# Writing out TensorE's order in the RWKV recurrence, the dilated attention and the gates of a two-block network

## The chip, the cores and the metric

The kernel runs on one core of a Trainium2 chip. The metric is the device time of one execution in microseconds (us). The kernel before has a median of 924.59 us over three runs (924.24 to 924.65).

## What is computed

The network maps 256 tokens of 1024 channels through two blocks. The first is an even layer (pooling and spatial gating) and an odd layer (gated linear attention and stick-breaking attention). The second block, where the change lies, is cut down here to its mixing part:

```python
u = rmsnorm_2(h, mix_pre_norm[i])
z = u @ w_in[i]
z_attn, z_rwkv, z_gate = ...
o_attn = dilated_attention_branch(z_attn)
o_rwkv = rwkv7_time_mix(z_rwkv, ...)
gate_attn, gate_rwkv = jnp.split(jax.nn.sigmoid(z_gate), 2, axis=-1)
merged = gate_attn * (o_attn @ w_attn_up[i]) + gate_rwkv * (o_rwkv @ w_rwkv_up[i])
h = h + rmsnorm_2(merged @ w_out[i], mix_post_norm[i])
```

`rwkv7_time_mix` is a recurrence over 256 steps for 8 heads of 64; after it come a feed-forward layer and a gated embedding (PLE), which the change leaves alone.

## The kernel before

Every dense product is done in three: a float32 weight tile of 128x1024 is split into a high part `whi` (ScalarE) and a low part `wlo` (VectorE), the activation likewise, and `acc_T` (line 398) issues high x high, high x low and low x high for each block of 128 channels. These three matmuls are called a gate step below when they belong to the gates. The gates need 16 tiles of 8 steps, 384 matmuls. A weight tile comes by a DMA of 512 KB on SP's queue (`weights`, line 367); there are three buffers each of `whi` and `wlo`, so a split also waits for the last matmul of the tile three before it.

The recurrence is done in four chunks of 64 tokens. `gram` (line 1645) makes 64x64 products of keys, queries and decay vectors, masked on VectorE into the tiles `G`. The chunk's triangular system is inverted by `inverse` (line 1809), for two groups of four heads: the innermost 16x16 blocks are solved in `bl` by a chain of small VectorE operations and come back through DRAM as `tb`; `tt` and its transpose `tn` are made from it on VectorE; then TensorE does tn x G, P1 x tt, and again on 32x32 blocks tn x G and tt x P1, with a copy of each result `P1` between. Then `rwkv` (line 1630) walks the four chunks: U, the state S, and on every second one the output Y, which is normalised, transposed and turned into the split tiles `mhl`.

The dilated attention (`attention`, line 1928) works for two query blocks j and two head pairs i: scores, a softmax (`sc`: exp, then scaling by the reciprocal sum, both on ScalarE), transposes of the weights, their copies `aPT`, and the product with the values into `o_ps`.

What sets the order: generators that yield after each piece, woven by ratios. Attention and gates are woven into `fill` by RA and RB, and `fill` into the recurrence by RC and RD (lines 239 and 1236). That is the order of issue only; each engine's program is then ordered by the scheduler from its own model. `keep_in_program_order` takes an instruction out of its hands, and is used for some operations elsewhere (`o`, line 311). After the recurrence, a loop (line 1239) does for each of 8 tiles 6 matmuls of attn_up and 12 of rwkv_up, and merges them under the gates.

## Time and profile before

| what | value |
| --- | --- |
| median of three runs | 924.59 us (924.24 to 924.65) |
| the profiled execution | 924.33 us |
| its span, first to last instruction | 922.6 us |
| mean granted TensorE clock, share of full speed | 0.986 |
| TensorE (PE) busy | 890.4 us, 97% of the span |
| VectorE (DVE) busy | 687.0 us, 74% |
| ScalarE (ACT) busy | 505.1 us, 55% |
| GpSimd (POOL) busy | 58.8 us, 6% |

The profiled execution's own time is 1.73 us longer than its span; this is what lies around the first and last instruction. PEld in the page is the loading of TensorE's weights, which overlaps its products. [...] All times of rows count from the start of the span.

## The change

TensorE's instructions of the recurrence, the attention and the gates are issued through `pe`, which keeps them in the order of the program while `first` is set. The generators' ratios go; instead `rwkv` calls `fill(a=, g=, u=)` by hand, which takes so many pieces of attention, of gates and of attn_up. A piece of the gates is one step (`gemm_fine`), and the next weight tile is asked for when a tile begins. It is `nc.tensor` calls beside `mm` that now go through `pe` too. The inverse yields after each half of its products, and two gate steps go there (one behind the last). Both head pairs' scores of a query block come first, then transposes and products; the product's accumulator comes from the other PSUM pool. attn_up moves into the loop of the last transposes, and the gate tile is overwritten in place.

```diff
-        self.nc.tensor.matmul(out, lhsT, rhs, start=start, stop=stop)
+        self.pe(self.nc.tensor.matmul(out, lhsT, rhs, start=start, stop=stop))
+
+    def pe(self, ins):
+
+        if self.first:
+            self.tc.keep_in_program_order(ins)
...
+    def gemm_fine(self, prefix, n, xs, evac):
+
+        w = self.weights(prefix + "0", NK)
+        for i in range(n):
+            acc = self.psum(T, prefix)
+            ahead = self.weights(prefix + str(i + 1), NK) if i + 1 < n else None
+            for k in range(NK):
+                self.acc_T(acc, w, xs[k:k + 1], 0, P, k0=k, first=k == 0, last=k == NK - 1)
+                if k == NK - 1:
+                    evac(i, acc)
+                yield
+            w = ahead
...
-        fill = self.weave(self.attention(qkv, o_at), self.gemm_T("gate", 16, us, ev_gate), RA, RB)
-        self.run(self.weave(self.rwkv(rw, o_rw), fill, RC, RD))
-        ms, wa = [], None
+        wa = []
+
+        def attn_up():
+
+            for i in range(8):
+                if i % 4 == 0:
+                    wa.append(self.weights("attn_up%d" % (i // 4), 2))
+                pa = self.psum(T, "up")
+                self.acc_T(pa, wa[-1], o_at, (i % 4) * P, (i % 4 + 1) * P)
+                self.stt(gates[i], gates[i], 1.0, pa, ALU.add, ALU.mult)
+                yield
+
+        att, gate, up = self.attention(qkv, o_at), self.gemm_fine("gate", 16, us, ev_gate), attn_up()
+
+        def fill(**n):
+            for g, name in ((att, "a"), (gate, "g"), (up, "u")):
+                for _ in range(n.get(name, 0)):
+                    next(g, None)
+
+        self.first = True
+        self.rwkv(rw, o_rw, fill)
+        fill(a=99, g=999, u=9)
+        self.first = False
...
-        yield from grams("ab", B, A, strict)
-        G = pre["ab"]
+        G = gram(B, A, strict)
...
-        for name, X, Y, mask in (("ak", K, A, strict), ("rb", B, R, causal)):
-            for _ in grams(name, X, Y, mask):
-                yield
-                yield
+        fill(a=2, g=4)
+        pre["ak"] = gram(K, A, strict)
+        fill(a=2, g=8)
+        fill(a=3)
+        pre["rb"] = gram(B, R, causal)
+        fill(g=4)
+        fill(a=1, g=4)
...
-            yield
-        for _ in range(NX):
-            yield
-        yield from self.weave(self.inverse(0, G, tb, TT[0]), self.inverse(1, G, tb, TT[1]), 1, 1)
+            fill(a=1, g=2)
+        fill(a=1, g=14)
+        for n, _ in enumerate(self.weave(*(self.inverse(hh, G, tb, TT[hh]) for hh in range(2)), 1, 1)):
+            fill(g=2 if n < 8 else 1)
...
-                yield
+                fill(g=3)
...
+                    if M is Kt:
+                        fill(g=2)
...
-            yield
+            fill(u=2)
...
         ps = self.pmisc((P, 8, 16))
         for m, g in M:
             for b in range(0, P, 32):
                 self.mm(ps[q(b), m, :], g[q(b), q(b % 64)], tn[q(b), m, 0:16], True, True)
+            if m % 4 == 3:
+                yield
...
+            s_of = []
             for i in range(2):
                 sc = self.b4("sc", 512)
                 ss = [sc[:, hh, 0:2 * n] for hh in range(2)]
-                mxs = scores(j, i, ss)
-                for hh in range(2):
-                    weights(ss[hh], mxs[hh])
-                    yield
-
-
+                for s, mx in zip(ss, scores(j, i, ss)):
+                    weights(s, mx)
+                s_of.append(ss)
+                yield
+            for i, ss in enumerate(s_of):
+
+
+                pts = []
                 for g in range(2):
                     nb, w = (2, m) if g else (j + 1, P)
                     ps = self.pmisc((P, 4, P))
                     bs = [(b, hh) for b in range(nb) for hh in range(2)]
                     for k, (b, hh) in enumerate(bs):
-                        nc.tensor.transpose(ps[0:w, k, :], ss[hh][:, g * n + b * w:g * n + (b + 1) * w], ident)
+                        self.pe(nc.tensor.transpose(ps[0:w, k, :], ss[hh][:, g * n + b * w:g * n + (b + 1) * w], ident))
                     pt = self.m2("aPT", (P, 4, P))
                     self.act(pt[0:w, 0:len(bs), :], ps[0:w, 0:len(bs), :])
+                    pts.append((pt, w, bs))
```

In the order of TensorE, at the start of the inverse (rwlev_pm is its accumulator, tn and P1 its operands, gate the accumulator of a gate tile), there stood before

```order
L309 MATMUL rwch_gate_1438_7390<-gla_hl_944_4590,rwch_wlo_1441_7394 128x256
L309 MATMUL rwlev_pm_1392_6999<-rwlev_tn_1389_6992,rwlev_G_1288_6464 32x16 x32
L309 MATMUL rwlev_pm_1394_7034<-rwlev_tn_1391_6996,rwlev_G_1289_6466 32x16 x32
L309 MATMUL rwlev_pm_1404_7110<-rwlev_P1_1393_7032,rwlev_tt_1388_6991 32x16 x32
L309 MATMUL rwlev_pm_1406_7146<-rwlev_P1_1395_7067,rwlev_tt_1390_6995 32x16 x32
L309 MATMUL rwlev_pm_1408_7182<-rwlev_tn_1389_6992,rwlev_G_1288_6464 32x32 x16
L309 MATMUL rwch_gate_1438_7390<-gla_hl_955_4645,rwch_whi_1440_7393 128x256 x2
L309 MATMUL rwlev_pm_1410_7206<-rwlev_tn_1391_6996,rwlev_G_1289_6466 32x32 x16
```

and now

```order
L309 MATMUL rwlev_gate_1414_7096<-gla_hl_955_4645,rwlev_whi_1411_7065 128x256 x2
L309 MATMUL rwlev_gate_1414_7096<-gla_hl_955_4645,rwlev_wlo_1412_7066 128x256
L309 MATMUL rwlev_pm_1420_7113<-rwlev_tn_1419_7110,rwlev_G_1288_6464 32x16 x16
L309 MATMUL rwlev_pm_1423_7134<-rwlev_tn_1422_7131,rwlev_G_1289_6466 32x16 x16
L309 MATMUL rwlev_gate_1414_7096<-gla_hl_968_4704,rwlev_whi_1411_7065 128x256 x2
L309 MATMUL rwlev_gate_1414_7096<-gla_hl_968_4704,rwlev_wlo_1412_7066 128x256
L309 MATMUL rwlev_gate_1414_7096<-gla_hl_981_4763,rwlev_whi_1411_7065 128x256 x2
L309 MATMUL rwlev_gate_1414_7096<-gla_hl_981_4763,rwlev_wlo_1412_7066 128x256
L309 MATMUL rwlev_pm_1420_7113<-rwlev_tn_1419_7110,rwlev_G_1288_6464 32x16 x16
L309 MATMUL rwlev_pm_1423_7134<-rwlev_tn_1422_7131,rwlev_G_1289_6466 32x16 x16
```

Four products of 32 rows that stood one behind the other are now eight of 16, with two gate steps behind each pair.

On VectorE, at the same place (gt is the evacuation of a finished gate tile, wlo the low part of a weight tile, tt and tn the operands of the inverse), there stood before

```order
L331 TENSOR_TENSOR rwlev_tt_1388_6991<-rwlev_tb_1356_6797,cst2_5133 128x256
L1823 STREAM_TRANSPOSE rwlev_tn_1389_6992<-rwlev_tt_1388_6991 128x256
L331 TENSOR_TENSOR rwlev_tt_1390_6995<-rwlev_tb_1356_6797,cst2_5133 128x256
L1964 RECIPROCAL rwlev_tn_1398_7073<-rwlev_tn_1397_7071 128x1
L1823 STREAM_TRANSPOSE rwlev_tn_1391_6996<-rwlev_tt_1390_6995 128x256
L331 TENSOR_TENSOR rwch_wlo_1472_7604<-rwch_wst_1470_7601,rwch_whi_1471_7603 128x1024
```

and now

```order
L336 TENSOR_TENSOR rwlev_gt_1413_7093<-rwlev_gate_1409_7062,rbc_u_5099 128x256
L336 TENSOR_TENSOR rwlev_tt_1418_7109<-rwlev_tb_1374_6843,cst2_5133 128x256
L1851 STREAM_TRANSPOSE rwlev_tn_1419_7110<-rwlev_tt_1418_7109 128x256
L336 TENSOR_TENSOR rwlev_tt_1421_7130<-rwlev_tb_1374_6843,cst2_5133 128x256
L336 TENSOR_TENSOR rwlev_wlo_1432_7278<-rwlev_wst_1430_7275,rwlev_whi_1431_7277 128x1024
L1851 STREAM_TRANSPOSE rwlev_tn_1422_7131<-rwlev_tt_1421_7130 128x256
```

An evacuation of a gate tile now stands ahead of the first tt, and a split of a weight tile between the second tt and its transpose.

On ScalarE, ahead of the last products of the inverse (P1 is their operand, TT the finished inverse), there stood before

```order
L343 ACTIVATE rwlev_TT_1284_6423<-rwlev_tt_1405_7144 32x8x32 x2
L343 ACTIVATE rwlev_P1_1409_7199<-rwlev_pm_1408_7182 32x256
L343 ACTIVATE rwlev_TT_1284_6423<-rwlev_tt_1405_7144 32x8x32 x2
L343 ACTIVATE rwlev_P1_1411_7223<-rwlev_pm_1410_7206 32x256
L343 ACTIVATE rwlev_TT_1285_6424<-rwlev_tt_1407_7180 32x8x32 x4
```

and now

```order
L348 ACTIVATE rwlev_TT_1285_6424<-rwlev_tt_1434_7291 32x8x32 x4
L348 ACTIVATE rwch_whi_1459_7487<-rwch_wst_1458_7485 128x1024
L348 ACTIVATE rwlev_gt_1437_7345<-rwlev_gt_1437_7345 128x256
L348 ACTIVATE rwlev_P1_1438_7348<-rwlev_pm_1435_7299 32x256
L348 ACTIVATE rwlev_P1_1440_7364<-rwlev_pm_1436_7308 32x256
```

The split whi_1459 and the tanh of a gate tile stand ahead of the two copies of P1. On VectorE the other half of the same place is now

```order
L336 TENSOR_TENSOR rwlev_gt_1437_7345<-rwlev_gate_1429_7274,rbc_u_5099 128x256
L336 TENSOR_TENSOR rwch_wlo_1460_7488<-rwch_wst_1458_7485,rwch_whi_1459_7487 128x1024
L1879 COPY rwlev_P1_1438_7348<-rwlev_pm_1435_7299 32x256
L1879 COPY rwlev_P1_1440_7364<-rwlev_pm_1436_7308 32x256
```

so that the low part of that same weight tile stands ahead of the copies into P1 there. The two splits write the buffers that gate tile 1429 reads, whose last matmul stands on TensorE directly ahead of tt x P1.

## Rows read from the trace of the kernel before

**Rows 1.** The page: TensorE's busy time, and its granted clock in 40 slices.

```profile
PE 890.4 (97%) x7228; PEld 828.3 (90%) x7228; DVE 687.0 (74%) x1284; ACT 505.1 (55%) x863; POOL 58.8 (6%) x120
...
PEclk7999999999999999999999999899999999999998
```

**Rows 2.** Windows: length, busy us of PE, PEld, DVE, ACT, POOL; clock, DMA share, GB/s.

```profile
588.00:590.00 2.00, 0.86 (x66) 0.65 (x65) 1.77 (x6) 1.25 (x2) 0.00 (x0) 1.00 0.80 233
...
592.00:594.00 2.00, 0.16 (x11) 0.16 (x13) 0.13 (x1) 0.83 (x2) 0.00 (x0) 0.95 0.83 248
594.00:600.00 6.00, 6.00 (x88) 5.65 (x84) 2.02 (x5) 4.25 (x10) 0.00 (x0) 0.50 0.02 5
600.00:602.00 2.00, 2.00 (x21) 1.69 (x21) 0.42 (x1) 0.78 (x1) 0.00 (x0) 0.84 0.00 0
```

**Rows 3.** All waits of TensorE, 540 to 672 us: total us, times, longest.

```profile
PE rwlev_pm L309 <- issue: 1.9, 1, 1.9
PE rwlev_pm L309 <- DVE rwlev_tn L1823: 1.1, 1, 1.1
PE rwlev_pm L1984 <- ACT rwlev_sc L343: 0.3, 1, 0.3
PE rwch_pm L1798 <- DVE rwch_Y L331: 0.3, 1, 0.3
```

**Rows 4.** TensorE's timeline, 578 to 602 us: start, length, operation, count, idle before.

```profile
578.53 2.08 PE L1643 MATMUL rwlev_pm<-rw_tok,rwlev_G 64*64 64x64 f32 x64
...
585.83 0.40 PE L309 MATMUL rwlev_gate<-gla_hl,rwlev_whi 128*128 128x256 f32 x2
...
586.19 0.40 PE L309 MATMUL rwlev_gate<-gla_hl,rwlev_whi 128*128 128x256 f32 x2
...
589.24 1.47 PE L309 MATMUL rwlev_pm<-rwlev_tn,rwlev_G 32*32 32x16 f32 x126 [1.10 <-DVE rwlev_tn L1823]
...
590.58 1.32 PE L309 MATMUL rwlev_pm<-rwlev_P,rwlev_tt 32*32 32x16 f32 x120
593.84 0.24 PE L309 MATMUL rwlev_pm<-rwlev_P,rwlev_tt 32*32 32x16 f32 x3 [1.95 <-issue]
...
595.59 1.07 PE L309 MATMUL rwlev_pm<-rwlev_tn,rwlev_G 32*32 32x32 f32 x32
...
597.71 0.63 PE L309 MATMUL rwch_gate<-gla_hl,rwch_whi 128*128 128x256 f32 x2
...
598.35 0.63 PE L309 MATMUL rwch_gate<-gla_hl,rwch_whi 128*128 128x256 f32 x2
...
601.94 1.20 PE L309 MATMUL rwlev_pm<-rwlev_tt,rwlev_P 32*32 32x32 f32 x64
```

**Rows 5.** VectorE's timeline, 588 to 596 us.

```profile
588.19 0.43 DVE L331 TENSOR_TENSOR rwlev_tt<-rwlev_tb,cst 128x256 f32<-128x256 f32 x1 [0.99 <-DMA rwlev_tb<-td]
588.65 0.45 DVE L1823 STREAM_TRANSPOSE rwlev_tn<-rwlev_tt 128x256 f32<-128x256 f32 x1
...
589.80 1.18 DVE L331 TENSOR_TENSOR rwch_wlo<-rwch_wst,rwch_whi 128x1024 fp32r<-128x1024 f32 x1
...
595.38 0.43 DVE L1847 COPY rwlev_P<-rwlev_pm 32x256 f32<-32x256 f32 x1 [0.42 <-ACT rwlev_P L343]
```

**Rows 6.** ScalarE's timeline, 583 to 599 us.

```profile
583.30 0.72 ACT L343 ACTIVATE rwlev_sc<-rwlev_sc,rwlev_tn 128x512 f32<-128x512 f32 x1 [2.05 <-DVE rwlev_tn L335]
...
584.88 1.06 ACT L343 ACTIVATE rwch_whi<-rwch_wst 128x1024 fp32r<-128x1024 f32 x1 [0.45 <-ACT rwlev_gt L343]
...
594.97 0.38 ACT L343 ACTIVATE rwlev_P<-rwlev_pm 32x256 f32<-32x256 f32 x1 [1.91 <-PE rwlev_pm L309]
...
598.81 0.60 ACT L343 ACTIVATE rwlev_aPT<-rwlev_pm 128x512 f32<-128x512 f32 x1
```

**Rows 7.** Around TensorE's wait in w_out: its row on the timeline, and the window.

```profile
688.86 0.39 PE L309 MATMUL rwch_w_out<-rwch_hl,rwch_wlo 128*128 128x256 f32 x1 [1.18 <-DVE rwch_wlo L331]
...
686.00:692.00 6.00, 4.82 (x41) 4.62 (x40) 5.65 (x11) 4.15 (x8) 0.00 (x0) 1.00 0.83 264
```

## What the change was predicted to do

> **What bounds the kernel now.** I read the page first: TensorE is busy for 890.4 of the 922.6 us, 97%, and the row of its granted clock is full in all slices but three [rows 1]. So time is won or lost only where TensorE waits, or where it works at its lower clock. The change touches only the stretch from about 549 us (first product of the recurrence) to the start of w_out. I therefore read that stretch by windows, then the list of TensorE's waits in it, then the timelines of TensorE, VectorE and ScalarE around the place where something is lost.

> The windows show one weak place, 588 to 602 us: in 588:590 TensorE has 0.86 us of work, in 592:594 only 0.16, and the clock is 0.50 in all of 594:600 [rows 2]. With the parts in 592:594 (0.95) and 600:602 (0.84) the half clock lasted 0.2 + 6.0 + 0.64 = 6.84 us. The waits name the rest: 1.1 us for a transpose of VectorE, 1.9 us put down to "issue", 0.3 for a scaled score tile, 0.3 for Y [rows 3]. Nothing else waits between 540 and 672. On TensorE's timeline these are the start of the 64x64 inverse at 589.24 (after 1.10), its 246 small products in two bursts without a gate between them, the 1.95 us before 593.84, and gate matmuls that come at half pace from 597.71 on [rows 4].

> **What goes away.** The total of TensorE's products does not change, only their order.
> - The two bursts (126 and 120 records, 589.24 to 591.9) are cut into pieces with two gate steps between them, so that TensorE no longer has hundreds of very short instructions in a row. I count the whole 1.95 us "issue" idle as gone; its bounds are 0 and 1.95. [...]
> - The 1.10 us wait for the transpose is replaced by the wait (c) below: 1.10 gone.
> - The 0.3 us wait for the scaled scores [rows 3]: gone, since the second pair of score products now stands ahead of the transposes.
> - The half clock. A gate step of three matmuls took 0.64 us there (597.71 to 598.35) and takes 0.36 at full clock (585.83 to 586.19) [rows 4]. In the 6.84 us TensorE did 17 gate matmuls (17/3 x 0.28 = 1.6 us lost) and two lots of 32 of the 32x32 products (1.07 per 32 at 595.59 against 1.20 per 64 at 601.94: 0.9), and four transposes, which I put at 0.3 as an estimate from the same ratio. That is 2.8; bounds 1.6 (gates alone) and 3.4 (half of 6.84).

> Together 1.95 + 1.10 + 0.3 + 2.8 = 6.2 us.

> **What the fixed order adds.** TensorE now runs in the written order, but VectorE and ScalarE still get theirs from the scheduler, and in it the splitting of the next gate weight tile often stands ahead of a small step of the inverse. The third weight buffer is free only when the last matmul of an earlier gate tile is done, so such a split is tied to TensorE's own progress.
> - (c) The first products of the inverse. On VectorE stand, behind the end of gate tile 1409: gt_1413, tt_1418, the transpose tn_1419, tt_1421, then wlo_1432, and only then the transpose tn_1422. By [rows 5] a tt is 0.43 and a transpose 0.45, and gt has the shape of tt: head 0's operand is there 1.3 us after the tile's end, while TensorE has two gate steps (0.72) to do: 0.6 wait. After these four VectorE has wlo_1432, 1.2 (whi_1431, 1.06 on ScalarE [rows 6], is done by then), and the transpose, 0.45: head 1's operand is there 1.3 + 0.3 + 1.2 + 0.45 = 3.25 after the tile's end (0.3 is the step of tt_1421, which overlaps). TensorE gets there at 0.72 + 0.6 + 0.3 = 1.6: another 1.6 wait. Sum 2.2; bounds 1.1 (as before) and 3.
> - (d) The last products of the inverse. whi_1459 waits for the last matmul of gate tile 1429, which is the instruction just ahead of tt x P on TensorE; P1_1438 needs both ScalarE, behind whi_1459, and VectorE, behind wlo_1460. So TensorE stands for whi 1.06 + wlo 1.2 + copy 0.43 = 2.7 us [rows 5, 6]. Nothing covers it. Bounds 1.4 (the ScalarE half alone: 1.06 + 0.38) and 3.2.
> - (b) The j = 1 product of attention, o, wants two aPT copies (0.60 each) on ScalarE, behind four exps and scales of the second score pair (0.72 each), whi_1411 (1.06) and two AKV copies (as large as aPT, 0.60 each) [rows 6]. From the end of the second score pair TensorE has 36 + 12 gate matmuls (5.8 us), the two halves of AKV (2.08 at 578.53) and eight transposes (an estimate of 0.8, a gate matmul's 0.12 each and a little less): 8.7. ScalarE has 4 x 0.72 + 1.06 + 4 x 0.60 = 6.3 of its own, and it starts only when VectorE has the maxima; the 2.05 us of idle before such a row [rows 6] is what that costs, with as much again between exp and scale. That is 10.4, so 1.7 more than TensorE has; bounds 0 and 3.
> - Two small ones: the second pair of scores waits for both G copies to free its accumulators, and the first rwkv_up product waits for its split operand: 0.7 together, bounds 0 and 1.5.
> - At no cost: the weight loads of SP are as many and in the same order, with three buffers, so each is issued when its buffer is free as before; attn_up (48 matmuls) only moves from behind the last transposes to between them, and what it covers there is the 0.3 wait for Y, which the new order still has ahead of the first transposes. If that cover were gone, 0.3 at each of the three later transposes.

> Added: 2.2 + 2.7 + 1.7 + 0.7 = 7.3.

> **The sum.** 924.33 us (profiled execution: span 922.6 and 1.73 around it) - 6.2 + 7.3 = 925.4. The profiled run lies 0.26 below the median of 924.59, so on the scale of the medians it is 925.7. A measurement of this kernel can tell about 0.2%, 1.85 us, from no change, so this is "same", near its upper edge. Its own spread by the bounds is some 2 us either way.

> **Rivals.**
> *The clock falls at the new stalls.* Before, it fell after 5.7 us (588.14 to 593.84) in which TensorE had only small products and two idle times (1.10 and 1.95) [rows 4], and did not at a plain idle time of 1.18 (688.86, clock 1.00 in 686:692) [rows 7]. The 2.7 of (d) is longer than any of these, and (c) makes 2.2 in three pieces with small products between. [...] Against it: at (c) and (d) full-size gate matmuls stand right before and after. One fall costs what it cost before, 2.8: 928.5; two, 931.3. It decides at one of the two stalls being long enough. Chance 0.27.

> *The waits are mostly covered: faster.* If ScalarE reaches the aPT copies in time (b = 0), if the split at (c) is done before head 1 asks (0.7 instead of 2.2), and if (d) is only the ScalarE half (1.4), the order adds 0.7 + 0.7 + 1.4 = 2.8 against 6.2 removed: 924.59 - 3.4 = 921.2. For it: before, VectorE idled 0.99 and ScalarE 2.05 around the same steps [rows 5, 6], so they have room. Against it: the two splits are tied to a matmul that stands directly ahead, so their chain can't start earlier. It turns on where these two splits stand when the weight buffer comes free. Chance 0.30.

> *The order is not what costs.* The stalls move only, and the inverse again waits about 3 us in all, with the half clock as before: 924.6. Chance 0.05. It would need the gate steps to make no difference between the bursts.

> **How the numbers follow.** Forecast 0.38, 925.7, own range 924 to 928. Faster by over 0.2% (below 922.7): most of the second rival and a little of the forecast, 0.30. Within: half of the forecast, the third rival and the edges of the others, 0.30. Slower (above 926.4): the rest of the forecast and nearly all of the first rival, 0.40. The range goes from 920.0 (the second rival less 1.2, about half the half clock's own bounds) to 930.0 (the first rival with one fall, plus 1.5 for the bounds of the waits).

> **What would show it.** In the profile after: no "issue" wait in the inverse; a wait of TensorE of some 1.6 us for the second transpose of the inverse, behind a wlo, and one for the copy of P1 of 2.7, both with the split of a gate weight directly ahead on VectorE; a wait of o for aPT of about 1.7. A clock row below 1.00 after either of the two long waits is the first rival. Waits of under 1 us at both, with the clock at 1.00, is the second. I am wrong altogether if TensorE's time is lost at a place that the list does not have, the state updates of the recurrence above all, where six gate matmuls (0.72 us) are to cover a copy of U.

## The result, and the profile after

Five executions of the changed kernel have a median of 931.95 us (929.96 to 935.16) against 924.24 (923.25 to 924.65): a ratio of 1.0085, 95% interval 1.0064 to 1.0106. It is slower, by 0.6 to 1.1%, and lies outside the stated range of 920 to 930. The profiled execution took 929.96 us with a span of 928.3, 5.7 more than before; it is the fastest of the five, so the median is 2 us above what the rows below hold.

The page of the kernel after, its first lines and the clock, to be set beside [rows 1]:

```profile
span 928.3 us, 18124 instructions
...
PE 893.6 (96%) x7228; PEld 830.5 (89%) x7228; DVE 684.2 (74%) x1284; ACT 503.8 (54%) x863; POOL 58.7 (6%) x120
...
PEclk9999999999999999999999999879999999999998
```

TensorE is busy for 3.2 us more with the same 7228 products, and idle for 2.5 us more. The loss lies between the last transposes ahead of the recurrence and the start of w_out; this stretch before, and then after (columns as in [rows 2]):

```profile
548.35:669.92 121.57, 117.62 (x1790) 108.05 (x1789) 82.27 (x210) 62.50 (x118) 6.71 (x12) 0.97 0.36 100
548.61:675.58 126.97, 119.97 (x1791) 110.18 (x1789) 79.27 (x208) 61.36 (x117) 6.67 (x12) 0.93 0.34 97
```

It is 5.4 us longer: 2.35 of it busy time, 3.05 idle time. The clock was lower there for longer:

```profile
580.00:590.00 10.00, 7.26 (x100) 6.48 (x98) 5.65 (x10) 5.84 (x12) 1.90 (x4) 1.00 0.51 129
590.00:600.00 10.00, 9.26 (x254) 8.58 (x254) 3.41 (x8) 4.00 (x9) 0.00 (x0) 0.66 0.20 57
600.00:610.00 10.00, 7.44 (x151) 6.43 (x150) 2.88 (x6) 4.08 (x10) 0.00 (x0) 0.84 0.34 107
610.00:620.00 10.00, 10.00 (x85) 9.01 (x85) 2.53 (x6) 2.55 (x4) 0.00 (x0) 0.65 0.01 2
620.00:630.00 10.00, 10.00 (x162) 9.23 (x161) 4.93 (x8) 3.15 (x5) 0.00 (x0) 1.00 0.33 98
```

The half clock lasted 2 x 10 x (0.34 + 0.16 + 0.35) = 17 us, against 6.84 before. The waits of TensorE from 540 to 685 us, in the place of [rows 3]:

```profile
PE rwlev_pm L309 <- DVE rwlev_tn L1851: 2.1, 2, 1.4
PE rwlev_pm L309 <- ACT rwlev_P L348: 1.8, 1, 1.8
PE rwlev_o L309 <- ACT rwlev_aPT L348: 1.1, 1, 1.1
PE rwlev_pm L309 <- DVE rwlev_P L1879: 0.8, 1, 0.8
PE rwlev_pm L309 <- ACT rw_tok L348: 0.4, 2, 0.3
PE rwlev_o L2034 <- ACT rwlev_aPT L348: 0.3, 1, 0.3
PE rwch_pm L309 <- DVE rwlev_AKV L336: 0.2, 1, 0.2
PE rwch_pm L1826 <- DVE rwch_Y L336: 0.2, 1, 0.2
```

These are the forecast's (c), (d) and (b), each within 0.3 us; "issue" is gone. On TensorE's timeline the two falls of the clock stand behind (c) and (d): gate steps come every 0.64 us from 595.65 and again from 607.61, as before from 597.71 [rows 4].

```profile
588.94 0.44 PE L309 MATMUL rwlev_pm<-rwlev_tn,rwlev_G 32*32 32x16 f32 x32 [0.70 <-DVE rwlev_tn L1851]
590.74 0.44 PE L309 MATMUL rwlev_pm<-rwlev_tn,rwlev_G 32*32 32x16 f32 x32 [1.36 <-DVE rwlev_tn L1851]
...
595.65 0.63 PE L309 MATMUL rwlev_gate<-gla_hl,rwlev_whi 128*128 128x256 f32 x2
...
605.06 0.24 PE L309 MATMUL rwlev_pm<-rwlev_tt,rwlev_P 32*32 32x32 f32 x2 [1.77 <-ACT rwlev_P L348]
606.09 0.78 PE L309 MATMUL rwlev_pm<-rwlev_tt,rwlev_P 32*32 32x32 f32 x30 [0.79 <-DVE rwlev_P L1879]
...
607.61 0.63 PE L309 MATMUL rwlev_gate<-gla_hl,rwlev_whi 128*128 128x256 f32 x2
```

w_out starts at 675.58 instead of 669.92: the whole difference is made before it. (In the listings of TensorE's order ahead of the prediction, x32 and x16 count matmuls: groups of 32 became groups of 16.)

## The experiments

All ratios are to the kernel before, run on the same chip; that one spread from 921 to 928 us there. The profile of each kernel is of one execution. Theory A: the splits of weight tiles that the scheduler put ahead of the inverse's small steps make the two long waits, and these drop the clock. B: cutting the small products up among gate steps drops it. C: the new order costs as a whole.

**Moving the tile boundaries by half a tile.** Where a split falls depends on which gate step ends a tile, so one number is enough.

```diff
-        fill(a=1, g=14)
+        fill(a=1, g=18)
```

> Only one number differs from the change: 18 gate steps instead of 14 stand between the attention's last product and the inverse, so every later tile boundary moves by half a tile; the count of products and of gate steps inside the inverse is the same. Theory A (the splits of weight tiles that stand ahead of the inverse's small steps make the two long waits, and the waits make the clock fall): the wait for the second transpose shrinks from 1.4 to about 0.8 us with none before it, the 2.6 us wait for P1 goes, the clock stays at 1.00 in 585 to 620, and the time is 919 to 922 us. Theory B (small products between gate steps, cut as the change cuts them, make the clock fall by themselves): the waits shrink as in A, but the clock still falls and the time is 925 to 929. Theory C (the loss lies in the order as a whole): 930 or more.

919.02 us (918.30 to 919.46), ratio 0.9936 (0.9920 to 0.9952): faster than before, with the same products and the same number of gate steps inside the inverse. Its waits and the windows of the inverse:

```profile
PE rwlev_o L309 <- ACT rwlev_aPT L348: 1.1, 1, 1.1
PE rwlev_pm L309 <- DVE rwlev_tn L1851: 0.7, 1, 0.7
PE rwlev_gate L309 <- issue: 0.6, 1, 0.6
```

```profile
590.00:596.00 6.00, 5.15 (x240) 4.54 (x241) 1.73 (x4) 1.88 (x4) 0.00 (x0) 1.00 0.47 136
596.00:602.00 6.00, 6.00 (x146) 5.32 (x135) 2.55 (x7) 5.00 (x12) 0.00 (x0) 1.00 0.13 47
602.00:608.00 6.00, 6.00 (x105) 5.42 (x105) 3.26 (x7) 3.33 (x7) 0.00 (x0) 1.00 0.30 90
608.00:614.00 6.00, 6.00 (x78) 5.29 (x77) 2.34 (x3) 1.81 (x4) 0.00 (x0) 1.00 0.30 89
```

Both long waits are gone and the clock does not fall in the inverse. B and C do not survive this. "Issue", which the change's list does not have, shows again, at 0.6. The stretch from the last transposes to w_out gives the price of the half clock, since the products are the same as in the change:

```profile
548.09:664.87 116.78, 112.95 (x1791) 103.70 (x1789) 79.60 (x208) 61.28 (x117) 6.69 (x12) 1.00 0.37 105
```

Busy time is 112.95 us at full clock, against 119.97 with 17 us at half clock: 7.0 us. It is also less than the 117.62 before, by more than the 3.4 us that 6.84 us of half clock can cost at most (an estimate, half of 6.84); so the new order by itself needs less busy time for the same products.

**Control: by a whole tile.** 22 steps instead of 14 bring the boundaries in the inverse back to where the change had them.

```diff
-        fill(a=1, g=14)
+        fill(a=1, g=22)
```

> 22 gate steps ahead of the inverse instead of 14: a whole tile more, so the tile boundaries inside the inverse stand where the change has them, with more cover ahead of it and eight steps fewer ahead of the last transposes. Theory A (where the splits fall decides): the waits of 0.7 + 1.4 and 2.6 us and both falls of the clock are back, and Y is waited for some 3 us at the end: 931 to 937 us. Rival (18 was better because it gave the inverse's operands more time): the waits stay as with 18 or shrink, 918 to 923.

939.08 us (934.69 to 940.90), ratio 1.0158 (1.0123 to 1.0193), above A's 937. The waits are back, 2.1 and 1.7 + 0.7, with 3.1 for Y, and so is the lower clock: it is 0.50 in 596:602, 602:608, 608:614 and 614:620. More time ahead of the inverse was not what helped. The wait for Y brought a further fall, directly behind full-size gate steps and one transpose:

```profile
660.16 0.27 PE L1826 MATMUL rwch_pm<-cst,rwch_Y 128*128 128x128 f32 x1
663.51 0.47 PE L1826 MATMUL rwch_pm<-cst,rwch_Y 128*128 128x128 f32 x1 [3.08 <-DVE rwch_Y L336]
...
664.00:666.00 2.00, 2.00 (x9) 1.82 (x9) 0.85 (x2) 0.96 (x2) 0.00 (x0) 0.50 0.60 231
```

**Holding back one split at a time.** In `gemm_fine`, `behind()` queues the split of one tile behind all that was issued before it; tile 8 is the one ahead of the second transpose, tile 10 the one ahead of P1.

```diff
-            ahead = self.weights(prefix + str(i + 1), NK) if i + 1 < n else None
+            with self.behind() if i + 1 in (8,) else ExitStack():
+                ahead = self.weights(prefix + str(i + 1), NK) if i + 1 < n else None
```

> The split of gate tile 8 (whi and wlo) is held behind all that was issued before it, so that it no longer stands ahead of the second transpose of the inverse; everything else as in the change. A: the first long wait falls from 0.7 + 1.4 to 0.7 + 0.5 us, the first fall of the clock goes, the wait for P1 (about 2.0 instead of 2.6, its split moves too) and the second fall stay: 925 to 928. B: both falls stay, 929 to 931.

926.39 us (922.76 to 932.19), ratio 1.0022 (1.0000 to 1.0045). The wait for the transposes is 1.1 instead of 2.1, that for P1 1.7 + 0.7; the first fall is gone and the second is there, for 13.7 us:

```profile
590.00:596.00 6.00, 6.00 (x249) 5.49 (x248) 2.69 (x6) 2.96 (x7) 0.00 (x0) 1.00 0.02 5
596.00:602.00 6.00, 3.63 (x81) 3.10 (x76) 3.22 (x6) 5.33 (x11) 0.00 (x0) 0.85 0.40 104
602.00:608.00 6.00, 6.00 (x78) 5.42 (x76) 1.58 (x3) 1.06 (x3) 0.00 (x0) 0.50 0.46 160
```

The same with (10,):

> The split of gate tile 10 alone is held back, so that it no longer stands ahead of the copies into P1. A: the wait for P1 falls from 2.6 to about 0.9 us and the second fall of the clock (10 us long, some 3 us of time) goes; the first wait of 0.7 + 1.4 and its fall stay: 925 to 928. B: both falls stay, 929 to 931.

924.05 us (920.29 to 927.76), ratio 0.9998 (0.9977 to 1.0019), just under the 925 expected. The wait for P1 fell to 0.8 as expected and the first fall stayed (0.59 in 592:594, 0.50 in 594:598), but in the profiled execution (927.67) the second was there too, among small products and gate steps:

```profile
603.52 0.78 PE L309 MATMUL rwlev_pm<-rwlev_tt,rwlev_P 32*32 32x32 f32 x30 [0.80 <-DVE rwlev_P L1880]
...
606.00:607.00 1.00, 1.00 (x8) 0.78 (x8) 0.76 (x2) 0.26 (x1) 0.00 (x0) 0.50 0.00 0
```

So A's claim that only the long waits do it is too strong: in this execution the clock fell behind a wait of 0.80 among small products. In the executions of this kernel the mean clock runs from 0.997 (in the fastest, 920.29) to 0.981 (in one of 927.51), so the falls are not the same in all of them.

**Idle time alone.** Starting from the 18-step kernel, the four gate steps between attention's transposes and its product go behind it (0 and 22 for 2 and 18), which leaves TensorE idle away from the inverse's 32-row products.

> As the kernel with 18, but the four gate steps between attention's transposes and its product stand behind that product: 0, 0 and 22 steps. The wait of o for aPT grows from 1.1 + 0.3 to about 2.5 + 0.6 us, idle time with full-size matmuls on both sides and no small products, while the inverse stays as it is there. If idle time of this length is enough to make the clock fall (as it fell about the 2.6 us wait in the change), the clock falls behind 580 us: 919.0 + 1.5 + about 3 = 923 to 925. If it takes the inverse's small products too, the clock stays and the time is 920 to 921.5.

922.73 us (920.30 to 924.82), ratio 0.9979 (0.9965 to 0.9993): 3.7 over the 18-step kernel. The inverse is as it was there, at 1.00; the clock fell at the wait for aPT (0.64 in 580:582, 0.50 in 582:586):

```profile
580.99 1.12 PE L309 MATMUL rwlev_o<-rwlev_aPT,rw_va 128*64 128x128 f32 x8 [2.52 <-ACT rwlev_aPT L348]
...
583.88 0.63 PE L309 MATMUL rwlev_gate<-gla_hl,rwlev_whi 128*128 128x256 f32 x2
584.52 0.63 PE L309 MATMUL rwlev_gate<-gla_hl,rwlev_whi 128*128 128x256 f32 x2
```

In this execution one idle time of 2.5 us was enough, without any of the inverse's products, and its 6.8 us of half clock made the stretch's busy time 115.62 instead of 112.95. By its mean clock of 0.997, as high as in the fastest executions of the kernel with 5, 5 and 12 below, the execution of 920.30 us had no such fall. Just ahead of the wait stand 64x64 products and transposes (575.07 to 578.46); what full-size matmuls directly ahead of it do is seen at Y's 3.08 us in the kernel with 22, where the clock fell too. The forecast's doubt, that full-size matmuls would keep the clock, is answered for that length and not for 2.5 us.

**Without pinning.** The change's issue order, TensorE's left to the scheduler.

```diff
-        self.first = True
+        self.first = False
```

> The change's order of issue, but TensorE's order is left to the scheduler (nothing is pinned); it puts the first products of the inverse later among the gates and in longer pieces. Theory A: what costs is not the issue order but that TensorE is held at the small products while the splits run; with the scheduler's order the two long waits go (o's wait of 1.4 stays), the clock falls at most once: 919 to 924. Rival C (the new order of attention, gates and attn_up costs by itself): 928 or more.

924.19 us (920.45 to 926.20), ratio 0.9999 (0.9982 to 1.0016). Both long waits are gone, but the small products stand in longer runs again, and the place of [rows 4] is back with its fall of the clock (0.87 in 590:596, 0.50 in 596:602):

```profile
594.89 0.94 PE L309 MATMUL rwlev_pm<-rwlev_P,rwlev_tt 32*32 32x16 f32 x55 [2.08 <-issue]
```

So the new order of issue costs nothing against before when TensorE's is left free; C falls a second time.

**Covering o's wait.** The boundaries as with 18, but the cover moved up.

```diff
-            fill(a=1, g=2)
-        fill(a=1, g=14)
+            fill(a=1, g=5)
+        fill(a=1, g=12)
```

> The boundaries of the gate tiles in the inverse stand as in the kernel with 18, but six of the gate steps ahead of it move up between attention's transposes and its product: 5 behind each AKV instead of 2, then 12. A: as there, and the wait of o for aPT (1.1 + 0.3 us) goes too: 1 to 2 us less than that kernel, 917.5 to 920.5. B: 924 to 928.

918.15 us (916.57 to 918.63), ratio 0.9924 (0.9907 to 0.9942); no wait of o is left. With 13 for 12:

> As the kernel with 5, 5 and 12 steps, with 13: one more gate step ahead of the inverse, which gives the split that still stands ahead of the second transpose 0.36 us more. Theory A: that wait falls from 0.8 to 0.4 and all else stays: 0.4 less, 917 to 918.5. If the split moves with it, 918 to 921.

917.92 us (917.12 to 920.62), ratio 0.9942 (0.9922 to 0.9961): not to be told from it. The wait for the transpose stayed at 0.7 and "issue" was 1.2. The kernel with 5, 5 and 12 is the better one to keep, 0.6 to 0.9% faster than before.

**Gate steps out of the inverse.** From that kernel, 29 steps ahead of the inverse and none in it.

> As the kernel with 5, 5 and 12 steps, but with no gate step inside the inverse: its 17 steps stand ahead of it. If long runs of very short products make the idle time called issue, 1 to 2.5 us of it appear inside the inverse (0.8 with the gates between), and the clock falls at least once, since there are small products and waits alone for some 8 us: 922 to 928. If the idle time has another cause, it is 0.8 or less; and if waits alone make the clock fall, it stays up, for no single wait here is over 0.5 us: 917 to 920.

926.05 us (923.49 to 928.20), ratio 1.0010 (0.9989 to 1.0031), some 8 us more than with the steps in it. "Issue" grows to 4.3 in two pieces:

```profile
594.38 0.42 PE L309 MATMUL rwlev_pm<-rwlev_P,rwlev_tt 32*32 32x16 f32 x27 [0.21 <-ACT rwlev_P L348]
598.40 1.57 PE L309 MATMUL rwlev_pm<-rwlev_P,rwlev_tt 32*32 32x16 f32 x101 [3.60 <-issue]
...
601.86 1.22 PE L309 MATMUL rwlev_pm<-rwlev_tn,rwlev_G 32*32 32x32 f32 x37 [0.74 <-issue]
```

"Issue" is 3.6 us more than with the steps in the inverse. Most of the rest is the clock: the lower one lasted 17 us here, and busy time from the last transposes to w_out is 117.09 against 112.75.

Where "issue" stands can be read from the traces, by counting TensorE's products and loads (the third and fourth columns) up to the pause: before, with 18 steps, and here up to the first and the second:

```profile
0.00:593.00 593.00, 573.42 (x4559) 529.34 (x4559) 454.91 (x827) 323.67 (x543) 56.35 (x118) 0.99 0.67 211
0.00:594.90 594.90, 575.81 (x4559) 531.07 (x4560) 455.23 (x834) 326.32 (x551) 56.12 (x118) 0.99 0.65 210
0.00:598.00 598.00, 578.06 (x4558) 534.10 (x4558) 456.99 (x836) 327.73 (x553) 56.20 (x118) 0.99 0.65 210
0.00:601.50 601.50, 580.76 (x4686) 536.46 (x4686) 458.34 (x840) 328.75 (x556) 56.20 (x118) 0.99 0.65 209
```

In all ten traces that show the pause it comes after 4558 or 4559 products and as many loads (at most one more), whether a small product or a gate step stands next; the second one here comes 256 records later. So it belongs to a place in TensorE's program and not to the run of products. The profile also has a DMA queue of kind "instruction", with 56 packets of 16 KB in the whole span. One of them lies in or just ahead of each of the ten pauses, here in the first:

```profile
q8 instruction: 1, 0.02, 1.6%
```

Its packet ends at 596.81, and TensorE goes on at 598.40; in the ten traces TensorE goes on 1.2 to 1.6 us after the packet's end. That the pause has to do with this packet is not shown: no run changed these packets alone. How long it is goes with how fast the 256 records ahead of the place were worked off, though not with that alone: 1.2 us before (pause 1.95), 2.0 here (3.60) and 2.1 with 13 steps (1.21), 2.6 in the kernels with 18 steps and with 5, 5 and 12 (0.55 and 0.77), and 4.3 in the change (none).

A further kernel, with one gate step behind each group of 32 small products, does not compute the same result, so its time is not set beside the others. Under 0.2 us of pause was expected if the length of the run makes it; it was 0.40, at the same place.

**attn_up behind the transposes again.** From the kernel with 5, 5 and 12, without `fill(u=2)`.

> As the kernel with 5, 5 and 12 steps, but attn_up stands behind the last transposes again and no longer between them. If attn_up covers the steps between two transposes, TensorE waits there 0.6 and about 1.2 us and the time rises by 1 to 2 us, to 919 to 920.5; if something else covers them, it stays within 0.5 of 918.2.

919.29 us (918.12 to 921.25), ratio 0.9955 (0.9939 to 0.9970), 1.1 us more in time and 0.3% by the ratios, whose intervals overlap. Only 0.4 of waits between transposes is in its profile, and its clock fell for 3.4 us in the inverse, ahead of any attn_up (0.83 in 590:596, after idle times of 0.69 and 0.66), where the other's did not. So the difference can't be put down to attn_up, and what attn_up is worth there stays open.

## Why the prediction was wrong

- **The waits it added were right.** (c) 2.2 forecast, 0.70 + 1.36 measured; (d) 2.7, and 1.77 + 0.79; (b) 1.7, and 1.10 + 0.32; the small ones 0.7, and 0.6, though not the ones named: the first products waited for rw_tok (0.4), and neither the second scores nor rwkv_up waited. In all 6.7 for 7.3.
- **The waits it removed were right in the sum.** 1.10, 1.95 and the 0.3 of the scores do not stand in the list after. But the 1.95 went along with the new waits: the change and the two kernels with one split held back keep at least one of them and show no pause, the pinned kernels with two gate steps behind each pair and no such wait show 0.55 to 1.21, and the one with 22, which has both, 0.7. Cutting the run is worth 0.7 to 1.4 (1.95 less 1.21 and less 0.55), not 1.95, since the pause keeps its place in TensorE's program.
- **The step that failed is the half clock.** The forecast booked 2.8 us as a gain and put a new fall into a rival, with 0.27 for one or two falls. The clock fell twice, for 17 us in place of 6.84. The price is 7.0 us against the same products at full clock, and at the same rate 2.8 before, so the forecast had the old fall right; but this term is not -2.8 but +4.2.
- **The rest of the miss.** The span is 928.3 against 923.7 (925.4 less 1.73), 4.6 more. The clock's 7.0 would give more than that. Against it stand 1.9 us less busy time that the new order needs at full clock (117.62 - 2.8 - 112.95, an estimate), which the forecast had at nothing, and 0.9 in the idle time of the stretch (3.05 more than before; 7.3 - 3.35 = 3.95 forecast); another 0.3 was lost ahead of the recurrence. It was the rival's case of two falls, 931.3, that came true.
- **Why the rival was priced too low.** The row it was judged by, 1.18 us idle at full clock [rows 7], is less than half of (d). Full-size matmuls next to the waits were held to speak against a fall, and the waits of 2.52 us (behind 64x64 products and transposes) and 3.08 (behind full-size ones) show falls all the same. (d) alone, at 2.7, lay beyond every row seen at full clock, so one fall should have been the forecast, and with (c) two the next likely.
- **The spread was missed as well.** The median is 2 us above the profiled execution. That the falls last differently long in different executions is likely but not shown, with one trace of each kernel: the mean clocks of the five, 0.979 to 0.987, do not order their times (0.979 is that of the median, 0.980 that of the slowest), and they take in a lower clock near the start that some executions have and that costs little (0.53 in 10:21 before, with 6.05 us busy, 1.00 after, with 5.86). Kernels whose profile shows no fall in the stretch spread by 1.2 to 3.5 us, those with one by 3.1 to 9.4 (4 to 10 executions each); the kernel before, which has one, by 1.4 beside the change and by 6.0 to 7.3 beside the experiments.
- **The rival on the other side was near what was possible:** with the splits elsewhere, its 921.2 became 919.0 and 918.2, by the mechanism it named (where the splits stand when the buffer comes free).

## What to carry to other kernels

Pinning one engine's order does not pin the engines that feed it: look at what the scheduler puts ahead of their short steps, above all a long operation that waits for the pinned engine itself. A wait that such a queue made cost more than its length here where TensorE's clock fell with it: 2.5 us of idle time cost 2.7 us more in the 6.8 us of half clock that came with it, and the two waits of the change cost 7.0 in 17. Where full-size work is cut into small steps, the position of its tile boundaries is a number to be tuned: 14, 18 and 22 steps at one place gave 932, 919 and 939 us.
